# Charging the weight split to the planner's later chains: one hybrid diffusion step on one core

## The chip, the cores and the metric

The kernel runs on one core of a Trainium2 chip. The metric is the device time of one execution in microseconds, the median of several runs.

## What is computed

One inference step of a two-layer network over 640 tokens (128 context tokens and 512 latent tokens) of width 1024. Each layer normalises its input, passes it through one wide input projection to four token mixers, merges their outputs with sigmoid gates, projects, adds, and ends with a SwiGLU network:

```python
h = _rmsnorm(x, norm1_g) * (1 + sc1) + sh1
(aq, ..., mg) = split(h @ w_in)
o_a = _gdn_mixer(...)          # gated DeltaNet, chunked, both directions
o_b = _diff_attend(q_b, keys, vals, lam)   # softmax(map 0) - lam * softmax(map 1)
o_c = _hgrn_mixer(...)         # gated linear recurrence, both directions
o_d = _na_latent(...)          # neighbourhood attention
proj = einsum('btnw,nwd->btnd', branches, w_branch)
x = x + g1 * (einsum('btnd,btnd->btd', sigmoid(mg), proj) @ w_out)
x = x + g2 * swiglu(rmsnorm(x, norm2_g) * (1 + sc2) + sh2)
```

All inputs and results are float32.

## The kernel before

**Products.** A dense product is made of three passes over halves of the numbers. `load_w` fetches a weight tile of 128x1024 numbers (`wraw`), ScalarE rounds it to `whi`, and VectorE subtracts to get the rest, `wlo`. A `unit` then issues three matmuls per 128 rows of the contraction: `whi` by the input's high part, `whi` by its low part, `wlo` by its high part. The inputs are `hh` and `hl` for the normalised input and `mo` for a mixer's output. Their results are the tiles `pu` (320 columns) and `ptk` (256 columns). This dense work is the **fill**.

**Chains.** The four mixers are long sequences of small steps in which TensorE, VectorE and ScalarE take turns. Each is a generator that yields the tiles that its next step on TensorE needs. The list of chains in order of urgency is `prep_a` (rank 0), `mix_a` (1), `mix_d` (2), `mix_c` (3), `mix_b` (4), `prep_b` (5) and `late` (6).

**The planner.** The order on TensorE (PE) is written out by hand. `weave` keeps a rough clock, `now`, of PE's modelled time. It runs a chain's step on PE when the clock has passed the time at which that step's inputs should be ready plus `SLACK` (220 ns); if no chain is due it runs the next piece of fill; if there is neither, the clock jumps. The ready times come from `charge`: each operation of a chain on VectorE or ScalarE adds its modelled cost to a modelled queue of its engine, one queue per rank, and pushes back the queues of all later ranks. The clock and the queues set positions only; no instruction waits for them on the chip.

**VectorE and ScalarE.** Their order is made by a scheduler from priorities. A chain's step has priority `100000 * (8 - rank)`, so 800000 to 600000 for ranks 0 to 2 and 500000 and less for the later ones. The split in `load_w` has `WPRI` = 550000, and stands between them.

**The end of a layer's woven part.** The last fill is `merge`, one per mixer: it multiplies that mixer's output with its part of `w_branch`. The merges come in the order `mix_a`, `mix_c`, `mix_b`, `mix_d`, each when its mixer is done, and `mix_a` and `mix_c` must both be done before the first. `mix_b` works through four heads. Of each head it takes five tiles of tokens (`b_tile`): scores of two maps (`pbs`, twice two rows), VectorE's maxima `b_mx`, ScalarE's exponentials into `be`, sums `b_s`, the combined weights `be` on VectorE, their transposes (`pbt` and the first `pbo`), copies, and the product with the values (the other `pbo`). After the fifth tile a norm (`bo`) and transposes (`goT`) follow, then the store to DRAM from which `merge` loads `moT` and splits it into `mo`.

Of the kernel before, what the change touches and what calls it, by code (L numbers as in the profile page):

```python
# [26 lines left out]
WAIT, WAIT1, FIX, LAT = 150.0, 300.0, 60.0, 270.0  # L27
# [85 lines left out]
class Net:  # L113
# [163 lines left out]
    def load_w(self, src, n=1024, pc=0, raw=None):  # L277

        if raw is None:
            raw = self.wraw.tile([128, 1024], F32, tag="raw", name="wraw")  # L280
        with self.tc.high_priority(offset=DPRI):
            self.nc.sync.dma_start(raw[:, :n], src)
        hi = self.whl.tile([128, 1024], F32R, tag="hi", name="whi")
        lo = self.whl.tile([128, 1024], F32R, tag="lo", name="wlo", bufs=NLO)
        with self.tc.high_priority(offset=WPRI):
            m = n - pc
            self.a.copy(hi[:, :n], raw[:, :n])
            self.v.tensor_tensor(lo[:, :m], raw[:, :m], hi[:, :m].bitcast(F32), ALU.subtract)
            if m < n:
                self.g.tensor_tensor(lo[:, m:n], raw[:, m:n], hi[:, m:n].bitcast(F32), ALU.subtract)  # L290
        return hi, lo
# [1663 lines left out]
```

## Time and profile before

| | |
|---|---|
| time of three runs, median (lowest to highest) | 3421.05 us (3419.64 to 3431.92) |
| the profiled execution, its own time | 3422.57 us |
| its span in the trace | 3420.8 us |
| PE busy in the span | 3325.7 us (97%) |
| VectorE (DVE) busy | 2315.1 us (68%) |
| ScalarE (ACT) busy | 1414.0 us (41%) |
| mean granted clock of TensorE | 0.99 |

PE is the engine to look at: it is busy in all but 95 us, so what the order can still change lies in its gaps and in the stretches in which its clock falls. The granted clock is 1.00 at 2.4 GHz and 0.50 at 1.2 GHz. The two layers' woven parts lie at about 100 to 1180 us and 1780 to 2860 us of the span; between and after them stand the output projection and the SwiGLU network, dense work almost without a gap.

### The profile page before, as it was taken

What the parts mean: (1) busy time and instruction counts of PE and PEld (TensorE: products, weight loads), DVE (VectorE), ACT (ScalarE), POOL (GpSimd) and SP (SyncE); (2) the same over time, 40 slices, a digit from 0 to 9 for tenths busy, and PEclk for the clock granted to TensorE, in tenths of its full rate; (3) what the DMA queues carried; (4) which work ended last, traced back from release to release, by engine and by line L of the source; (5) the groups of instructions that cost most, each with busy time, mean ns of one, the idle gap of its engine ahead of it and who ended that gap; (6) DMA issues with size and microseconds to landing.
All of it is one profiled execution on the core that took longest, in us unless ns stands there. A gap on an engine that the chain in (4) does not pass through costs nothing.

```text
span 3420.8 us, 62210 instructions
## 1 busy us (share of the span) xinstructions
PE 3325.7 (97%) x23732; PEld 3257.6 (95%) x23732; DVE 2315.1 (68%) x5237; ACT 1414.0 (41%) x3162; POOL 222.5 (7%) x385
## 2 busy tenths in 40 slices
PE   8999999999999899999999999999999998999998
PEld 5999999999999899999999999999999998999998
DVE  7689788866666577887456887677556656633435
ACT  5344545545444352222253545555444433422222
POOL 1010000120000000000001101002100100000000
PEclk9999999999999999999999999999999999999999
DMA  6454434675443444544234433356544425322222
GB/s 223 161 167 127 142 125 146 187 226 163 133 138 114 125 157 144 152 152 132 83 122 155 147 124 106 121 147 208 166 123 132 129 70 164 102 70 75 78 77 69
DMA packets 288131, 460.08 MB, mean 134 GB/s; under 512 B 47060, under 2 KB 174676, under 8 KB 287832
## 3 DMA queue, kind: packets, MB, share of 16 engines
q1 hardware_dynamic: 276504, 423.58, 40.0%
q0 software_dynamic: 11328, 32.52, 3.2%
q8 instruction: 187, 3.06, 0.4%
q14 instruction: 112, 0.92, 0.1%
HBM read 368.42 MB, written 87.56 MB: 133 GB/s over the span
## 4 chain that ended last, share of the span: by engine, by line
PE 82%; DVE 7%; DMA 4%; issue 3%; ACT 2%; POOL 1%; SPq 0%; DVEq 0%; ACTq 0%; POOLq 0%
PE pu L151 60%; PE ptk L151 5%; PE pdv L151 1%; PE pW L151 1%; PE pX L151 1%; PE pbs L151 1%; PE pca L151 1%; PE pbo L151 1%; PE pkS L151 1%; PE pdt L157 1%; DVE wlo L106 1%; PE pds L151 1%; PE pao L151 1%; DVE cacc L106 1%; DMA bqk<-rr 1%
## 5 line engine op out<-in xcount | busy, mean ns | idle before, releaser
L151 PE MATMUL pu<-hh,whi 128*128 128x320 f32 (+1 forms) x3760 | 1091.9, 318 | 8.3 <-ACT stg L106 5.1
L151 PE MATMUL pu<-hl,whi 128*128 128x320 f32 (+1 forms) x3760 | 1060.8, 310 | 2.4 <-DVE hl L106 2.4
L151 PE MATMUL pu<-hh,wlo 128*128 128x320 f32 (+1 forms) x3760 | 1061.8, 310 | 0.0
L106 ACT CAST whi<-wraw 128x1024 fp32r<-128x1024 f32 (+2 forms) x410 | 390.5, 953 | 893.8 <-PE pu L151 573.4
L151 PEld LDWEIGHTS pu<-hh,whi 128*128 128x128 f32 (+1 forms) x3760 | 680.1, 188 | 12.7 <-ACT stg L106 5.3
L151 PEld LDWEIGHTS pu<-hl,whi 128*128 128x128 f32 (+1 forms) x3760 | 680.2, 188 | 4.5 <-DVE hl L106 2.6
L151 PEld LDWEIGHTS pu<-hh,wlo 128*128 128x128 f32 (+1 forms) x3760 | 678.9, 187 | 1.7
L106 DVE TENSOR_TENSOR wlo<-wraw,whi 128x1024 fp32r<-128x1024 f32 (+2 forms) x410 | 453.7, 1107 | 299.6 <-ACT whi L106 296.9
L151 PE MATMUL pu<-mo,whi 128*128 128x320 f32 x1024 | 236.7, 319 | 9.6 <-ACT mo L106 9.0
L151 PE MATMUL pu<-fa,whi 128*128 128x320 f32 x1152 | 215.6, 309 | 0.0
L106 DVE SCALAR_TENSOR_TENSOR x<-pu,gn,x 128x128 f32<-128x128 f32 (+1 forms) x336 | 134.0, 434 | 94.0 <-PE pu L151 93.1
L151 PE MATMUL ptk<-whi,hh 128*128 128x256 f32 x640 | 191.2, 299 | 0.0
L151 PEld LDWEIGHTS pu<-mo,whi 128*128 128x128 f32 x1024 | 173.2, 192 | 11.2 <-ACT mo L106 9.7
L151 PE MATMUL ptk<-wlo,hh 128*128 128x256 f32 x640 | 181.5, 284 | 0.5 <-DVE wlo L106 0.5
L151 PE MATMUL ptk<-whi,hl 128*128 128x256 f32 x640 | 181.5, 284 | 0.0
L151 PEld LDWEIGHTS pu<-fa,whi 128*128 128x128 f32 x1152 | 180.8, 188 | 0.0
L151 PE MATMUL pu<-mo,wlo 128*128 128x320 f32 x512 | 160.4, 313 | 0.0
L151 PE MATMUL pu<-fa,wlo 128*128 128x320 f32 x576 | 131.2, 309 | 0.0
L511 DVE CUSTOM_DVE_ANT_0 junk<-wa,cs,bada 128x512 bf16<-128x512 f32 x160 | 120.7, 754 | 5.3 <-DMA wa<-in_wada 2.8
L151 PEld LDWEIGHTS ptk<-wlo,hh 128*128 128x128 f32 x640 | 123.1, 192 | 0.7 <-DVE wlo L106 0.7
L511 DVE CUSTOM_DVE_ANT_0 junk<-wa,cs,mod 128x512 bf16<-128x512 f32 x160 | 119.5, 747 | 5.9 <-DMA wa<-in_wada 3.5
L106 DVE TENSOR_TENSOR fs<-fs,pu 128x320 f32<-128x320 f32 x88 | 39.6, 483 | 123.8 <-PE pu L151 123.8
(422 smaller groups left out, 5924.5 us busy)
## 6 DMA issues: line engine op xcount, KB each, us to landing
wraw<-in_win SPq DMA_DIRECT2D x151, 512.0 KB, 3.8
wa<-in_wada SPq DMA_DIRECT2D x180, 256.0 KB, 3.0
wraw<-in_wg SPq DMA_DIRECT2D x44, 512.0 KB, 3.5
wraw<-in_wu SPq DMA_DIRECT2D x44, 512.0 KB, 3.6
wraw<-in_wd SPq DMA_DIRECT2D x80, 256.0 KB, 2.7
p<-stg SPq DMA_DIRECT2D x112, 160.0 KB, 2.6
wraw<-in_wtok SPq DMA_DIRECT2D x32, 512.0 KB, 3.7
wraw<-in_wbr SPq DMA_DIRECT2D x32, 512.0 KB, 3.5
```

The lines of the kernel that those rows point to most:

```text
L106: r = f(*args, **kw)
L151: r = self.nc.tensor.matmul(out, lhsT, rhs, start=start, stop=stop)
L157: r = self.nc.tensor.transpose(out, src, ident)
L511: self.nc.vector.tensor_tensor_reduce(junk, raw, cs[g], 0.5, o if k0 else self.bada[:, l, m:m + 1], ALU.mult, ALU.add, o)
```

## The change

Every weight tile that is loaded while the planner runs now pushes the modelled queues of ScalarE and VectorE for the ranks 3 to 7, that is for `mix_c`, `mix_b`, `prep_b` and `late`. The costs are the model's own: 60 + 0.84 n ns on ScalarE and 60 + 1.04 n ns on VectorE for n columns. Nothing is added on any engine; the number of instructions stays as it is, and only places move.

```diff
         hi = self.whl.tile([128, 1024], F32R, tag="hi", name="whi")
         lo = self.whl.tile([128, 1024], F32R, tag="lo", name="wlo", bufs=NLO)
+        if self.weaving:
+
+            for key, ns in (('a', 0.84), ('v', 1.04)):
+                q = self.free.setdefault(key, [0.0] * 8)
+                for r in range(3, 8):
+                    q[r] = max(q[r], self.now) + FIX + ns * n
         with self.tc.high_priority(offset=WPRI):
             m = n - pc
             self.a.copy(hi[:, :n], raw[:, :n])
```

**First place: PE at the end of `mix_b` in the first layer**, the last tile of the last head (`pbs` scores, `pbt` and `pbo` transposes, `pbo` values, `goT` transposes of the finished head; `pu` is fill). Before:

```order
L157 MATMUL pbt<-cst_119,be 128x128 x4
L157 MATMUL pbo<-cst_119,be 128x128 x2
L151 MATMUL pu<-mo,whi 128x320 x2
L151 MATMUL pu<-mo,wlo 128x320
...
L151 MATMUL pbo<-bv,be 128x128 x4
L151 MATMUL pbo<-bcx,be 128x128 x2
L151 MATMUL pu<-mo,whi 128x320 x2
L151 MATMUL pu<-mo,wlo 128x320
...
L157 MATMUL goT_13898<-cst_119,bo 128x128
L157 MATMUL goT<-cst_119,bo 128x128 x4
```

And now:

```order
L151 MATMUL pbs<-bKd,bqt 128x512 x2
L151 MATMUL pbs<-bKc,bqt 128x256 x2
L151 MATMUL pbs<-bKd,bqt 128x512 x2
L151 MATMUL pbs<-bKc,bqt 128x256 x2
L157 MATMUL pbt<-cst_119,be 128x128 x4
L157 MATMUL pbo<-cst_119,be 128x128 x2
L151 MATMUL pbo<-bv,be 128x128 x4
L151 MATMUL pbo<-bcx,be 128x128 x2
L157 MATMUL goT_13898<-cst_119,bo 128x128
L157 MATMUL goT<-cst_119,bo 128x128 x4
```

In the order before, the tile's two pairs of scores had 36 matmuls of fill between them, then 60 until `pbt`, 15 until the values and 12 until `goT`. Now the fill has run out: nothing stands between any of these steps. The tile before it has lost its cover too: 15 matmuls between its two pairs of scores, and none until its `pbt` and its values. `goT` itself stands where it stood: in both orders the merges of `mix_a`, `mix_c` and `mix_d` are ahead of it, and only `mix_b`'s own merge is behind.

**Second place: PE at the same end in the second layer.** Before:

```order
L157 MATMUL pbt<-cst_119,be 128x128 x4
L157 MATMUL pbo<-cst_119,be 128x128 x2
L151 MATMUL pu<-mo,whi 128x320 x2
L151 MATMUL pu<-mo,wlo 128x320
...
L151 MATMUL pbo<-bv,be 128x128 x4
L151 MATMUL pbo<-bcx,be 128x128 x2
L151 MATMUL pu<-mo,whi 128x320 x2
L151 MATMUL pu<-mo,wlo 128x320
...
L157 MATMUL goT_33081<-cst_119,bo 128x128
L157 MATMUL goT<-cst_119,bo 128x128 x4
```

And now:

```order
L151 MATMUL pbs<-bKd,bqt 128x512 x2
L151 MATMUL pbs<-bKc,bqt 128x256 x2
L151 MATMUL pbs<-bKd,bqt 128x512 x2
L151 MATMUL pbs<-bKc,bqt 128x256 x2
L157 MATMUL pbt<-cst_119,be 128x128 x4
L157 MATMUL pbo<-cst_119,be 128x128 x2
L151 MATMUL pbo<-bv,be 128x128 x4
L151 MATMUL pbo<-bcx,be 128x128 x2
L157 MATMUL goT_33081<-cst_119,bo 128x128
L157 MATMUL goT<-cst_119,bo 128x128 x4
```

Before, 15 matmuls of fill stood ahead of the values and 24 ahead of `goT`. Now only this last tile stands bare; the tile before it keeps 60 matmuls until its `pbt` and 6 until its values.

**Third place: PE at the end of `mix_d` in the first layer** (`pdt` are the transposes of its weights, one block per head; `pbt` and `pbo` belong to a tile of `mix_b` beside it). Before:

```order
L157 MATMUL pdt<-cst_119,dPl 128x128
L157 MATMUL pdt<-cst_119,dPl 96x128
L157 MATMUL pbt<-cst_119,be 128x128 x4
L157 MATMUL pbo<-cst_119,be 128x128 x2
L151 MATMUL pu<-mo,whi 128x320 x2
L151 MATMUL pu<-mo,wlo 128x320
```

And now:

```order
L157 MATMUL pdt<-cst_119,dPl 128x128
L157 MATMUL pdt<-cst_119,dPl 96x128
L157 MATMUL pbt<-cst_119,be 128x128 x4
L157 MATMUL pbo<-cst_119,be 128x128 x2
L151 MATMUL pbo<-bv,be 128x128 x4
L151 MATMUL pbo<-bcx,be 128x128 x2
```

Before, 21 matmuls of fill stood ahead of the last scores, 21 between these and the first head's `pdt`, and 15 between it and the second head's. Now there is none from the scores on until `mix_d` is done, as it nearly was in the second layer already before the change.

## Rows read from the trace of the kernel before

**Rows 1.** The page, span and first part: busy us, share, instructions.
```profile
span 3420.8 us, 62210 instructions
...
PE 3325.7 (97%) x23732; PEld 3257.6 (95%) x23732; DVE 2315.1 (68%) x5237; ACT 1414.0 (41%) x3162; POOL 222.5 (7%) x385
```

**Rows 2.** Five stretches: us, engines' busy us (instructions), PE clock, DMA share, GB/s.
```profile
200.00:400.00 200.00, 188.19 (x1472) 183.04 (x1471) 176.12 (x378) 97.49 (x222) 16.58 (x30) 0.99 0.44 142
...
1050.00:1100.00 50.00, 47.09 (x332) 46.27 (x331) 30.05 (x78) 18.45 (x46) 0.10 (x1) 1.00 0.37 105
1150.00:1180.00 30.00, 21.41 (x120) 20.50 (x119) 15.54 (x39) 8.20 (x17) 0.00 (x0) 0.77 0.40 123
...
2720.00:2750.00 30.00, 25.07 (x161) 23.23 (x160) 17.98 (x60) 13.99 (x41) 8.51 (x15) 0.89 0.49 143
2830.00:2860.00 30.00, 21.36 (x137) 20.32 (x136) 17.90 (x43) 9.96 (x19) 0.00 (x0) 0.89 0.47 139
```

**Rows 3.** What PE waited for: total us, times, longest us.
```profile
PE goT L157 <- DVE bo L106: 9.8, 3, 5.5
PE pu L151 <- ACT mo L106: 9.0, 2, 6.0
PE pdt L157 <- ACT dPl L106: 6.2, 2, 4.1
...
PE pdt L157 <- DVE b_nm L106: 4.8, 1, 4.8
...
PE pab L157 <- DVE atok L106: 3.9, 2, 2.2
PE pkS L151 <- DVE xp L106: 3.6, 3, 2.0
PE pW L151 <- DVE GT L106: 3.5, 8, 1.4
...
PE pco L151 <- DVE cSS L106: 2.3, 2, 2.1
PE pX L151 <- ACT W L106: 2.1, 2, 1.8
...
PE pbo L151 <- DVE be L106: 1.6, 2, 1.0
```

**Rows 4.** In order of time: the first layer's last `mix_b` tile (start us, us).
```profile
1143.92 0.40 PE L151 MATMUL pbs<-bKc,bqt 128*128 128x256 f32 x2
...
1147.67 1.02 DVE L106 SCALAR_TENSOR_TENSOR be<-be,b_c 128x768 f32<-128x768 f32 x1
...
1152.96 0.60 PE L157 MATMUL pbt<-cst,be 128*128 128x128 f32 x4
```

**Rows 5.** In order of time: a `mix_b` tile without fill, second layer.
```profile
2718.63 1.05 PE L151 MATMUL pbo<-bv,be 128*128 128x128 f32 x8
...
2724.05 0.40 PE L151 MATMUL pbs<-bKc,bqt 128*128 128x256 f32 x2
...
2730.34 1.00 PE L157 MATMUL pbt<-cst,be 128*128 128x128 f32 x4 [1.05 <-DVE be L106]
...
2731.14 0.64 PE L157 MATMUL pbo<-cst,be 128*128 128x128 f32 x2
...
2732.38 2.05 PE L151 MATMUL pbo<-bv,be 128*128 128x128 f32 x8 [0.61 <-DVE be L106]
```

**Rows 6.** In order of time: values to `goT`, first layer, then second.
```profile
1156.71 0.61 PE L151 MATMUL pbo<-bcx,be 128*128 128x128 f32 x4
...
1164.62 1.33 PE L157 MATMUL goT<-cst,bo 128*128 128x128 f32 x5 [5.54 <-DVE bo L106]
...
2834.80 0.61 PE L151 MATMUL pbo<-bcx,be 128*128 128x128 f32 x4
...
2841.07 0.77 PE L157 MATMUL goT<-cst,bo 128*128 128x128 f32 x5 [2.13 <-DVE bo L106]
```

## The prediction, as it was put on record

> **What bounds the kernel now.** I read the page first: PE is busy 3325.7 of 3420.8 us [rows 1], so 95 us of gaps are all that an order can win outright. Then the busy time by stretches. From 200 to 400 us VectorE works 176 of 200 us, and PE loses 12 us of gaps: there the chains wait for VectorE. At the end of `mix_b` the loss is denser: 8.6 of 30 us idle at 1150, at a mean clock of 0.77, and 8.6 of 30 at 2830, at 0.89. The ends of `mix_d` differ: 2.9 of 50 us idle in the first layer at full clock, 4.9 of 30 us in the second, at 0.89 [rows 2]. Then PE's list of waits, which says whose step was late, and last the order of time at the two ends.
>
> The list splits by rank. `pab`, `pkS`, `pW` and `pX` are steps of the ranks 0 and 1: 3.9 + 3.6 + 3.5 + 2.1 = 13.1 us. The change does not charge them. Of the ranks 3 and 4 there is `pco` with 2.3, `pbo` with 1.6 and `goT` with 9.8 us; of `goT`'s three waits the two at the layers' ends are 5.54 and 2.13 us, which leaves 2.1 [rows 3, 6]. So the steps that the change moves later waited some 6 us in all away from the ends. That is the whole direct prize.
>
> **Does a late rank need more time?** One tile shows it. In the first layer's last tile the second scores end at 1143.92 + 0.40 = 1144.32, and the weights are written at 1147.67 + 1.02 = 1148.69: 4.4 us. PE takes up its `pbt` at 1152.96, another 4.3 us later [rows 4]. The 60 matmuls of fill in between took these 8.6 us together, twice what was needed. A later place for such a step removes no wait. It spends fill that is wanted elsewhere.
>
> **The change part by part.** No instruction is added or taken away. The splits stay as they are; the code alone moves steps on PE, and with them what the schedulers of VectorE, ScalarE and the DMA queues put beside them. I cost the last at nothing while dense fill covers them; without fill it counts in the waits below.
>
> *End of `mix_b`, first layer.* Its steps come later while the fill ends where it did, so the last one and a half tiles stand bare.
> - The fourth tile's weights: 4.4 us from the second scores [rows 4] with no fill: 4.4 us idle.
> - Its copies between the transposes and the values: a bare tile waited 0.61 us [rows 5]: 0.6.
> - The fifth tile: both scores stand together, so its two maps queue on VectorE and ScalarE. A tile with its scores side by side and no fill shows 2724.05 + 0.40 to 2730.34, that is 5.9 us [rows 5], though `mix_d`'s last steps ran within it. The single chain's 4.4 us is the lower bound, 5.9 the value and the upper one: 5.9 idle, and again 0.6 for the copies.
> - The norm: from the values' end to `goT` 7.3 us (1157.32 to 1164.62) in the first layer and 5.7 (2835.41 to 2841.07) in the second; in both, work of the merges sits between its small steps on VectorE. Now the fill ends earlier and less of that work is left, so I take 5.7, with 7.3 as the other bound. The 5.54 us of idle before [rows 6] become 5.7: 0.2 more.
>
> Together 4.4 + 0.6 + 5.9 + 0.6 + 0.2 = 11.7 us.
>
> *The same end, second layer.* Only the fifth tile is bare: 5.9 + 0.6, and `goT` goes from 2.13 to 5.7, 3.6 more. Together 10.1 us. What is late behind `goT` in both layers is the store and the load of `mo`, 9.0 us in two waits [rows 3]; both start from `goT`, and I leave them as they are.
>
> *Clock in these ends.* A bare tile also runs slowly: its eight value matmuls took 2.05 us against 1.05 with fill around them [rows 5], the granted clock at 1.2 instead of 2.4 GHz. A tile's other matmuls lose about as much again, so about 2 us a tile, and three tiles give 6 us. The lower bound is nothing (the clock may fall only after them), the upper is 6 plus some 4 us at each end in which the fill behind restarts at 1.2 GHz.
>
> [...]
>
> *End of `mix_d`, first layer.* It becomes what the second layer's end is already: 4.9 us idle in place of 2.9, and a clock of 0.89 over 30 us, 6.6 us at half speed [rows 2], most of it with small matmuls, some 2 us. Together 4; bounds 0 and 6. The second layer's end keeps its form.
>
> *What is won.* The later places end the waits of `pco` and the part of `pbo` outside that end: 2.3 + 1.0 = 3.3 us [rows 3]; `goT`'s 2.1 is already in the account of `mix_d`'s end. Then there is an indirect gain: where VectorE is full (88% of 200 to 400 us), `mix_c`'s work comes some microseconds later and makes room for `prep_a` and `mix_a`. Nothing in the trace before shows how much. The bounds are 0 (these ranks already go first) and all 13.1 us; I take a quarter, 3.3, since they have the higher priority and lose mainly to what has already begun. With 1.4 us for the clock that falls after such gaps this is 8 us; bounds 0 and 3.3 + 13.1 + 1.4 = 18.
>
> *Sum.* 11.7 + 10.1 + 6 + 4 - 8 = 23.8 us. The profiled execution took 3422.57 us, 1.8 more than its span, so 3446.4; it stands 1.5 above the median of the runs, and the forecast is 3445 us.
>
> **Rivals.**
> *Even.* The two ends cost the lower bounds (10.2 and 8.6 us with 4.4 for each tile), the clock in them nothing, `mix_d`'s end nothing, and the middle wins 12: 3421 + 7 = 3428. For it: much of VectorE's load is `mix_c`'s. Against it: the clock at 1150 and 2830 is already low with fewer bare steps.
> *The middle pays it all.* One mechanism: VectorE's full stretches, 200 to 400 us and their like in the second layer. If moving `mix_c` out of them ends the 13.1 us of the ranks 0 and 1, their low clock (0.99 of 200 us, 4 us at half speed, in each layer some 2 us) and the 5.4 us of `pco`, `pbo` and `goT`, and `pdt`'s 6.2 + 4.8 us of `mix_d` [rows 3] go too, 13.1 + 4 + 5.4 + 11.0 = 33.5 us are won against 18.8 lost at the lower bounds: 3406, not slower. It decides from 19 us won, and from 36 it is a gain of over 0.5%. Against it: these chains already precede the others on VectorE.
> *The charge does not do what it says.* It is laid on the queues when a piece of fill begins in the program, while the split is done whenever a buffer comes free, some weights ahead. Then chains move later at places where no split is in their way, the waits in the middle stay, and the restart at low clock comes on top: 3421 + 32 + 8 = 3461. For it: the twofold cover in the tile above.
>
> **How the numbers follow.** The forecast has 0.53, the even case 0.25, the charge that misses 0.13, the middle that pays it all 0.09. About 0.5%, 17 us, is what can be told from no change here: 3404 to 3438. Slower by more than that are the forecast, but for a sixth of it that falls under 3438, and the third rival: 0.44 + 0.13, with a twentieth from the edge of the even case 0.60. Faster is what of the last rival lies beyond 3404, 0.06; 0.34 is left within. The range: the lower bounds of all losses, 18.8, against 18 won give 3422, and with the edge of the last rival 3416; the upper ones, 26.5 for the ends (5.9 for each bare tile, 7.3 for the norm), 14 for the clock and 6, with nothing won, give 3467. I give 3416 to 3465; the likeliest case alone has 3434 to 3460.
>
> **What would show it.** Each step has a place. Right: at both `mix_b` ends `pbt` waits 4 to 6 us for `be`, `goT` waits over 5 us, the granted clock over those 30 us falls below the 0.77 and 0.89 of before, and PE's idle time over the span rises by 10 to 25 us. `mix_d`'s first end looks like the second. Wrong: `pbt` does not appear among PE's waits, or the idle time from 200 to 400 us falls below 6 us. If the ends cost what I say and the time still stays, the middle paid, and PE's list will show `pab`, `pkS` and `pW` gone.

## The result, and the profile after

The changed kernel took 3475.33 us (median of four runs, 3473.89 to 3481.76) against 3421.22 before: a ratio of 1.0153, with a 95% interval of 1.0139 to 1.0168. It is 54 us slower. The forecast was 24 us slower, and the measured time lies 10 us above the end of its range. One execution of the last experiment below ran at a mean clock of 0.65 (4643 us) and is left out of its figures.

The profiled execution of the changed kernel took 3481.76 us, 6 more than its median; the profiles below are of that one. The page, span and first part:

```profile
span 3480.0 us, 62253 instructions
...
PE 3348.9 (96%) x23732; PEld 3276.3 (94%) x23732; DVE 2320.2 (67%) x5237; ACT 1418.5 (41%) x3164; POOL 214.8 (6%) x385
```

Against [rows 1] the span is 59.2 us longer. PE's idle time went from 95.1 to 131.1 us, 36.0 more, and its busy time rose by 23.2 us for the same 23732 matmuls. Over the span the mean granted clock fell from 0.990 to 0.984. The work of VectorE and ScalarE is the same within 5 us.

Busy time by stretches, the columns as in [rows 2], at the places that answer to those rows (the program runs later here, so the stretches do too):

```profile
200.00:400.00 200.00, 190.79 (x1502) 185.91 (x1501) 171.71 (x367) 97.59 (x224) 16.05 (x30) 1.00 0.45 145
1050.00:1100.00 50.00, 45.53 (x297) 43.57 (x297) 32.69 (x87) 20.27 (x53) 9.74 (x17) 0.90 0.39 113
1165.00:1210.00 45.00, 25.50 (x121) 22.95 (x119) 20.57 (x57) 12.18 (x35) 0.00 (x0) 0.73 0.21 67
2755.00:2785.00 30.00, 21.26 (x145) 19.18 (x144) 19.04 (x62) 13.94 (x42) 6.69 (x13) 0.89 0.34 102
2880.00:2915.00 35.00, 20.36 (x99) 18.57 (x98) 16.43 (x45) 10.06 (x26) 0.00 (x0) 0.76 0.31 96
```

At the end of `mix_b` PE is idle 19.5 of 45 us in the first layer and 14.6 of 35 in the second, where it was 8.6 in each [rows 2]. The end of `mix_d` got worse in both layers: 4.5 us idle at a clock of 0.90 in the first, 8.7 of 30 us in the second, which was forecast to stay at 4.9. From 200 to 400 us PE is idle 9.2 us in place of 11.8, and VectorE has 4 us less to do there: an indirect gain may be there, and it is small.

What PE waited for, columns as in [rows 3]:

```profile
PE pbt L157 <- DVE be L106: 20.6, 6, 6.2
PE pds L157 <- ACT dP L106: 10.7, 5, 4.0
PE goT L157 <- DVE bo L106: 7.9, 2, 4.0
...
PE pu L151 <- ACT mo L106: 6.8, 2, 3.5
PE pck L157 <- ACT ckd L106: 5.7, 1, 5.7
PE pco L151 <- DVE cSS L106: 5.3, 3, 3.9
...
PE ppv L151 <- DVE GX L106: 3.6, 1, 3.6
PE pCT L157 <- DVE C L106: 3.4, 1, 3.4
```

`pbt`, the wait that the forecast named, leads the list. But `pco`, which was to go, grew from 2.3 to 5.3. The wait for `dP` of `mix_d`, 1.0 us before, is 10.7, and `ckd` of `mix_c` (5.7 us) and `ppv` and `pCT` of `mix_a` (3.6 and 3.4) are new in the list.

The first layer's last two tiles of `mix_b`, in order of time:

```profile
1170.05 0.40 PE L151 MATMUL pbs<-bKc,bqt 128*128 128x256 f32 x2
...
1171.19 1.22 DVE L106 TENSOR_TENSOR wlo<-wraw,whi 128x1024 fp32r<-128x1024 f32 x1
...
1172.91 1.29 DVE L106 TENSOR_TENSOR mo<-moT,mo 128x320 fp32r<-128x320 f32 x3
...
1176.47 1.09 PE L157 MATMUL pbt<-cst,be 128*128 128x128 f32 x4 [6.02 <-DVE be L106]
...
1178.60 2.05 PE L151 MATMUL pbo<-bv,be 128*128 128x128 f32 x8 [0.61 <-DVE be L106]
...
1183.43 0.63 PE L151 MATMUL pbs<-bKc,bqt 128*128 128x256 f32 x2
...
1189.05 1.08 PE L157 MATMUL pbt<-cst,be 128*128 128x128 f32 x4 [5.00 <-DVE be L106]
...
1191.17 2.05 PE L151 MATMUL pbo<-bv,be 128*128 128x128 f32 x8 [0.61 <-DVE be L106]
...
1198.04 1.33 PE L157 MATMUL goT<-cst,bo 128*128 128x128 f32 x5 [3.96 <-DVE bo L106]
```

Read down the brackets: 6.02 + 0.61 + 5.00 + 0.61 + 3.96 = 16.2 us of idle time. The forecast had 4.4 + 0.6 + 5.9 + 0.6 + 5.7 = 17.2. That the sums are so near is in part luck: the fourth tile took 1.6 us more than forecast, the fifth 0.9 and the norm 1.7 less. In the 6.02 us of the fourth tile VectorE also did 3.9 us of work for the fill (the split `wlo`, parts of `mo`, a step of the merge); in the 5.00 us of the fifth it had none.

### The profile page after: what moved, and what is told of

It reads as the page before. It is cut to its first block, busy times and chain, and to the rows that moved or that the text cites. A ratio compares the mean times of both kernels' runs of the same rounds, so it can differ in the third digit from the quotient of the medians.

```text
span 3480.0 us, 62253 instructions
## 1 busy us (share of the span) xinstructions
PE 3348.9 (96%) x23732; PEld 3276.3 (94%) x23732; DVE 2320.2 (67%) x5237; ACT 1418.5 (41%) x3164; POOL 214.8 (6%) x385
## 4 chain that ended last, share of the span: by engine, by line
PE 78%; DVE 8%; DMA 5%; issue 4%; ACT 3%; POOL 1%; SPq 1%; DVEq 0%; ACTq 0%; POOLq 0%
PE pu L151 58%; PE ptk L151 4%; PE pdv L151 2%; PE pbo L151 1%; PE pbs L151 1%; PE pW L151 1%; PE pX L151 1%; PE pca L151 1%; DVE wlo L106 1%; PE pkS L151 1%; PE pdt L157 1%; DVE cacc L106 1%; PE pds L151 1%; PE pao L151 1%; ACT whi L106 1%
## 5 line engine op out<-in xcount | busy, mean ns | idle before, releaser
L517 DVE CUSTOM_DVE_ANT_0 junk<-wa,cs,mod 128x512 bf16<-128x512 f32 x160 | 119.6, 748 | 10.8 <-DMA wa<-in_wada 8.6
L151 PEld LDWEIGHTS ptk<-whi,hh 128*128 128x128 f32 x640 | 122.5, 191 | 0.0
```

The source lines that it names most:

```text
L151: r = self.nc.tensor.matmul(out, lhsT, rhs, start=start, stop=stop)
L517: self.nc.vector.tensor_tensor_reduce(junk, raw, cs[g], 0.5, o if k0 else self.bada[:, l, m:m + 1], ALU.mult, ALU.add, o)
```

## The experiments

To see where a kernel loses, I numbered the dense matmuls (`pu` and `ptk`), whose sequence is the same in all kernels, and compared the times at which the same ones start. The table gives the loss (or, with a minus, the gain) against the profile of before, in us, by stretches. In the profile of before they are: up to 1018 us, the end of `mix_d` (to 1119), the end of `mix_b` (to 1212), and for the second layer up to 2636, 2803 and 2893 us. The last column is the loss at the last dense matmul. A step of a chain that is moved from one stretch to another takes its PE time along: a tile moved out of an end shows as a loss in the middle, and a tile moved into an end as a gain in the middle. So the 0.1 and 1.1 of the changed kernel hide a loss; the sum is free of this.

| kernel | layer 1 up to there | `mix_d` end | `mix_b` end | layer 2 up to there | `mix_d` end | `mix_b` end | sum |
|---|---|---|---|---|---|---|---|
| changed kernel | 0.1 | 10.0 | 22.3 | 1.1 | 11.6 | 14.9 | 59.9 |
| charge in layer 1 only | -1.7 | 9.2 | 23.6 | -2.3 | -0.4 | 1.1 | 29.5 |
| rank 3 only | 4.4 | 9.4 | 2.8 | 7.3 | 9.6 | 5.0 | 38.5 |
| rank 4 only | 1.1 | 2.6 | 9.6 | -6.1 | 7.8 | 7.1 | 22.0 |
| changed kernel, PE kept busy | -2.2 | 9.3 | 19.5 | 1.8 | 10.9 | 12.1 | 51.2 |
| half the charge | 4.6 | -1.0 | 13.7 | 2.0 | -1.7 | 2.5 | 20.6 |
| ranks 4 up 50 ns earlier | 9.5 | -5.8 | -12.9 | -3.6 | 5.2 | -10.0 | -17.6 |
| ranks 4 up 100 ns earlier | 10.8 | -5.9 | -16.0 | -1.4 | 2.9 | -13.1 | -22.9 |
| ranks 4 up 200 ns earlier | 42.6 | -12.4 | -15.5 | 18.0 | -5.4 | -12.9 | 14.0 |
| ranks 3 up 100 ns earlier | 11.7 | -9.0 | -15.7 | 7.9 | 10.9 | -12.6 | -6.5 |
| changed kernel, ranks 4 up 150 ns earlier | 11.2 | 4.2 | -13.1 | 8.1 | 6.6 | -12.3 | 4.6 |

**The charge in the first layer only.**

```diff
-        if self.weaving:
+        if self.weaving and self.layer == 0:
```

> The charge is laid in the first layer only. Theory A (the fill runs out before the last steps of mix_d and mix_b, and each layer pays at its own ends): the first layer pays as in the changed kernel, where the same matmuls of fill run 32 us later after the layer's end than before, and the second layer is as before; 3421 + 26 to 32 = 3447 to 3453 us, and the order of time after 1800 us is that of the kernel before, shifted. Theory B (the delay of VectorE, ScalarE and the loads is carried through the program): the second layer loses too although its order is the old one; 3460 to 3475 us.

Measured: 3452.56 us, ratio 1.0079 (1.0064 to 1.0095). Theory A's range, and B is out. The first layer pays 31 us as in the changed kernel; the second runs as before. The first layer's `mix_b` end, and the stretches that answer to the second layer's `mix_d` and `mix_b` ends of [rows 2]:

```profile
1165.00:1210.00 45.00, 25.25 (x110) 22.84 (x109) 20.26 (x56) 12.77 (x36) 0.00 (x0) 0.70 0.20 63
2749.00:2779.00 30.00, 25.07 (x164) 23.24 (x163) 18.04 (x60) 14.35 (x43) 8.51 (x15) 0.89 0.50 143
2859.00:2889.00 30.00, 21.96 (x128) 20.64 (x128) 17.22 (x42) 9.34 (x19) 0.00 (x0) 0.77 0.46 132
```

The first end is as bare as in the changed kernel. The second layer's ends have 4.9 and 8.0 us idle, as before the change (4.9 and 8.6); only the clock at the last one is lower, 0.77 in place of 0.89.

**Rank 3 only.**

```diff
-                for r in range(3, 8):
+                for r in (3,):
```

> Only rank 3 (mix_c) is charged. Theory A: mix_b's last tile keeps 33 and 42 matmuls of fill ahead of its pbt (4.8 and 6.2 us against 4.4 needed), so little idle there; goT stands bare, about 0.2 and 3.6 us more than before, the copies 0.6 each, the clock some 2; mix_d's ends lose most of what they lost in the changed kernel (10 and 12 us), some 15 to 20 in all. 3440 to 3448 us. Theory C (the loss comes from mix_c's delay, which holds up the event late and with it all merges by 138 matmuls): as slow as the changed kernel, 3468 to 3480 us. Theory D (mix_b's delay alone makes the loss): no change, 3418 to 3426 us.

Measured: 3463.94 us, ratio 1.0113 (1.0098 to 1.0128), between A and C. A's part on the ends holds: in the table `mix_b`'s cost 2.8 and 5.0 us and `mix_d`'s 9.4 and 9.6. What A did not have is the rest: 12 us lost along the way. PE's waits:

```profile
PE pbt L157 <- DVE be L106: 12.4, 5, 4.4
...
PE pds L157 <- ACT dP L106: 8.0, 5, 3.3
...
PE pCT L157 <- DVE C L106: 3.8, 1, 3.8
```

`pds` is a step of `mix_d` (rank 2) and `pCT` one of `mix_a` (rank 1); neither is charged. `pds` waited 1.0 us before and now waits 8.0, and `pCT`, which was not in the list, 3.8. `pbt` of `mix_b`, not charged here either, went from 1.1 to 12.4, most of it at `mix_d`'s ends and in the second layer's middle. A delay of `mix_c` costs other chains.

**Rank 4 only.**

```diff
-                for r in range(3, 8):
+                for r in (4,):
```

> Only rank 4 (mix_b) is charged. Theory A: mix_b's last tile keeps 12 and 27 matmuls of fill ahead of its pbt (1.8 and 4.0 us against 4.4), so 2.6 and 0.4 us idle, 0.6 for the copies twice, goT 0.2 and 3.6 more, the clock some 3 to 5; mix_d's ends are nearly those of before. 3430 to 3438 us. Theory C (mix_c's delay and late): no change, 3418 to 3426 us. Theory D (mix_b's delay alone): as the changed kernel, 3468 to 3480 us.

Measured: 3444.48 us, ratio 1.0056 (1.0041 to 1.0071): 6 us above A's range, far from C and D. With rank 3 alone at 39 and rank 4 alone at 20 us the two make 59, about the 54 of both. So neither chain is the cause by itself. But they do not cost the same things: in the middles rank 4 adds next to nothing, as the idle times in the part on the prediction show.

**The opposite edit.** The kernel before, with a constant that its model already has:

```diff
-RW, RK = 0.0, 4
+RW, RK = -100.0, 4
```

> The kernel before with the opposite edit: the ranks from 4 on are modelled 100 ns faster for each operation (RW = -100), so mix_b's steps come earlier on PE and 240 and 225 matmuls of fill are left after its last step. Theory A: the waits at mix_b's ends (goT 5.5 and 2.1 us, mo 3.1 and 6.0 us) and the clock that falls there go; the tiles have 4.3 us in hand, so no new waits in the middle: 3395 to 3408 us. The theory that the places before were right for the middle, and that any shift costs there: 3425 us or more.

Measured: 3403.55 us, ratio 0.9939 (0.9922 to 0.9956): faster than both kernels. The two `mix_b` ends gain 16 and 13 us. The first of them, and of the list of waits the longest and `pbt`:

```profile
1140.00:1170.00 30.00, 28.08 (x178) 27.27 (x177) 15.08 (x28) 9.71 (x17) 0.00 (x0) 0.94 0.51 160
```

```profile
PE pdt L157 <- DVE dPl L106: 6.8, 1, 6.8
...
PE pbt L157 <- DVE be L106: 3.3, 2, 2.2
```

1.9 us idle in 30, against 8.6 at this end before [rows 2]; `goT` is gone from the head of the list.

**Keeping PE busy in the bare places.** The changed kernel, with matmuls whose result nobody reads wherever the planner's clock jumps:

```diff
                 assert first is not None, "chains wait for each other"
+                k = int(0.35 * (first - self.now) / 147)
+                if k:
+                    ps, x = self.G1("warm"), self.h[0][0]
+                    for _ in range(k):
+                        self.nc.tensor.matmul(ps[:, :HT], x[:, :128], x[:, :HT], start=True, stop=True)
                 self.now = first
```

> The changed kernel; wherever the planner's clock jumps because nothing is due, PE also runs some matmuls on the normalised input into a tile that nobody reads (about 0.35 of the jump long, some 230 in all, 34 us, in places where PE idled 50 us). They do no useful work. Theory A1 (at the bare ends the clock costs as much as the idle time: in the changed kernel 48.9 us more at 1.2 GHz and 23.2 us more of PE busy for the same matmuls): the ends stay at 2.4 GHz, the time at half clock falls by 30 us or more, and the time is 10 to 20 us under the changed kernel's: 3455 to 3467 us. Theory A2 (the idle time alone decides, or the added matmuls delay the chain's steps as much as they save): 3472 to 3485 us.

Measured: 3473.22 us, ratio 1.0147 (1.0131 to 1.0164), not to be told from the changed kernel's 1.0153. That is A2's range and not A1's, though the clock did what A1 said: over the first layer's end it rose from 0.73 to 0.92.

```profile
1160.00:1205.00 45.00, 36.55 (x230) 34.36 (x229) 22.34 (x60) 13.59 (x37) 0.00 (x0) 0.92 0.25 79
```

The order of time there shows why:

```profile
1167.92 0.40 PE L151 MATMUL pbs<-bKc,bqt 128*128 128x256 f32 x2
1168.16 2.81 PE L227 MATMUL warm<-hh 128*128 128x320 f32 x18
1174.04 0.63 PE L157 MATMUL pbt<-cst,be 128*128 128x128 f32 x4 [3.08 <-DVE be L106]
...
1179.17 1.62 PE L227 MATMUL warm<-hh 128*128 128x320 f32 x10
1180.63 0.63 PE L151 MATMUL pbs<-bKd,bqt 128*128 128x512 f32 x2
...
1192.82 0.76 PE L157 MATMUL goT<-cst,bo 128*128 128x128 f32 x5 [0.61 <-DVE bo L106]
```

From the end of the scores (1168.32) to `pbt` it is 5.7 us, against 6.0 without the added matmuls, at mean clocks of 0.92 and 0.73 over this end: most of this tile's time is VectorE's and ScalarE's. And the ten matmuls between the two pairs of scores put the second pair off by 1.5 us, so that part of what the tile's own matmuls gain at the higher clock (its four `pbt` took 0.63 us in place of 1.09) is given back. From this `pbt` to `goT` it is 18.8 us against 21.6, and in the table each `mix_b` end is 2.8 us shorter. So at each bare end the higher clock, less the delays, is worth some 3 us in these two profiles; over the whole kernel the medians differ by 2 us, which the intervals do not tell from none.

**Half the charge.**

```diff
-                    q[r] = max(q[r], self.now) + FIX + ns * n
+                    q[r] = max(q[r], self.now) + 0.5 * (FIX + ns * n)
```

> The charge at half its size. Theory A (what counts is which of the last steps stand bare): in the first layer mix_b's last tile alone is bare, with two pieces of fill between its scores, in the second layer the end is nearly as before; mix_d's ends are as before; 12 to 18 us at the first end and 2 to 4 at the second: 3435 to 3443 us. Theory P (the loss grows evenly with the charge, since each step is put off by as much): half of 54, 3446 to 3451 us.

Measured: 3439.08 us, ratio 1.0043 (1.0030 to 1.0056): A's range, and under P's. The table has 13.7 and 2.5 us at the two `mix_b` ends, as A said. Under a third of the loss (0.0043 of 0.0153) for half of the charge: it does not grow evenly with the charge, and fits what A says, that it counts which steps are left without fill. A did not have all of it: the longest waits of this run are two of the fill in the middles for `stg`, 11.4 and 6.3 us, where the kernel before waited 5.1 once.

**The opposite edit, twice the size.**

```diff
-RW, RK = 0.0, 4
+RW, RK = -200.0, 4
```

> As the earlier mirror edit, but 200 ns in place of 100 for ranks 4 and up. Theory A: the ends are already covered with 100 ns, so nothing more is won there; mix_d's ends move little. Steps of mix_b come so early that some begin to wait in the middle: 3400 to 3412 us. Theory P (evenly, the other way): another 20 us less than with 100 ns, 3378 to 3388 us.

Measured: 3436.50 us, ratio 1.0038 (1.0025 to 1.0051). Both theories miss. `mix_b`'s ends gain what they gained with 100 ns, as A said; outside them the kernel loses far more than A allowed:

```profile
PE pbt L157 <- DVE be L106: 13.1, 11, 3.8
PE pbt L157 <- DVE grs_y L106: 7.5, 1, 7.5
```

Now `pbt` waits twelve times, none of them at `mix_b`'s last tiles: the 4.3 us in hand [rows 4] were those of one tile late in the layer, and other tiles had less. That a busier VectorE is why was not looked into.

**The opposite edit for `mix_c` too.**

```diff
-RW, RK = 0.0, 4
+RW, RK = -100.0, 3
```

> As the mirror edit with 100 ns, for ranks 3 and up, so that mix_c comes earlier too (its last step after 3999 matmuls of fill in the first layer in place of 4143, 13867 in place of 14462 in the second). Theory A: the first mix_d end, too, is covered better, and the merges start earlier: 3395 to 3405 us, unless mix_c, whose steps take turns with mix_a on a full VectorE from 200 to 400 us, now waits there: then 3405 to 3420 us, with pco, pca or pcs in PE's list of waits.

Measured: 3420.71 us, ratio 0.9988 (0.9977 to 0.9999): A's second case, at the end of its range; nearly all of the gain of 21 us is gone, with longer waits of `mix_c` and of `mix_a` beside it.

```profile
PE pco L151 <- DVE cSS L106: 8.9, 3, 7.2
PE pkS L151 <- DVE xp L106: 7.5, 6, 2.4
PE pab L157 <- DVE atok L106: 6.3, 3, 2.8
```

`pkS` and `pab` had 3.6 and 3.9 us [rows 3]. So the ranks 0 and 1 do lose when `mix_c` comes earlier; that it is VectorE they lose on fits the list, which names it as what they waited for.

**Repair of the ends alone.** The changed kernel with `RW, RK = -150.0, 4`.

```diff
-RW, RK = 0.0, 4
+RW, RK = -150.0, 4
```

> The changed kernel with 150 ns taken off each operation of the ranks from 4 on, so that the charge stays on mix_c but mix_b catches up: 108 and 219 matmuls of fill are left after its last step. Theory A (mix_b's bare ends are the largest part, 27 us of idle time and clock against the kernel before, and another 17 us that the kernel before loses there itself; the rest, in the middle and at mix_d's ends, comes from mix_c's delay and stays): 3425 to 3440 us. Theory E (the loss in the middle also comes from mix_b's places): 3400 to 3412 us. Theory F (the ends matter little): over 3460 us.

Measured: 3426.53 us, ratio 1.0010 (1.0000 to 1.0021): A's range. With `mix_b`'s ends covered again (2.0 and 2.1 us idle) the changed kernel is as fast as before; but it is 23 us slower than the kernel that has the cover, by 100 ns, and no charge. In the table the two differ at `mix_d`'s ends and in the second layer's middle, and little at `mix_b`'s ends. The waits of `pck` and `pds` are those of the charged kernels again, and `pbt` waits at `mix_d`'s ends and in the first layer's middle:

```profile
PE pbt L157 <- DVE be L106: 13.1, 5, 5.1
PE pck L157 <- ACT dPl L106: 7.7, 2, 6.9
PE pds L157 <- ACT dP L106: 6.3, 3, 4.1
```

**The opposite edit at half its size.**

```diff
-RW, RK = 0.0, 4
+RW, RK = -50.0, 4
```

> The mirror edit with 50 ns in place of 100; 105 matmuls of fill are left behind mix_b's last step in each layer. Theory A (the ends need some 7 us of fill behind goT and no more): as with 100 ns, 3398 to 3410 us. Theory P (evenly with the size): half of that gain, 3411 to 3417 us.

Measured: 3404.18 us (median of three), ratio 0.9944 (0.9923 to 0.9964), not to be told from 100 ns: A's range, not P's. Here 105 matmuls behind the last step bought what 240 and 225 did.

## Why the prediction was wrong

**The direction and the main mechanism held.** The fill runs out before `mix_b`'s last steps, PE waits in each of them, and each layer pays by itself. Of the signs that were named, `pbt` waited 5.0 to 6.2 us at both ends and the clock fell to 0.73 and 0.76; `goT` stayed under its 5 us, and the rise in idle time, 36.0 us, is above the 10 to 25. In the first layer the idle time grew by 10.9 us (8.6 to 19.5); the forecast was 11.7. In the second it grew by 6.0 against 10.1: `goT` waited 3.96 us there too, not 5.7, since with the fill gone nothing stood between the norm's small steps on VectorE (first layer, 1194.9 to 1198.0 us), and the wait for `mo` fell as well, 9.0 to 6.8 us for both layers.

**The step that failed first is "What is won".** It was put down as 8 us gained (6.6 of it idle time), with 0 as its lower bound. It is a loss. PE's idle time in the middles went from 16.5 to 22.5 us in the first layer and from 11.2 to 19.3 us in the second, 14 us more, while `pab` and `pkS` did get better (3.9 to 0.6 and 3.6 to 2.2 us). Both middles, before and after:

```profile
333.00:1018.00 685.00, 668.46 (x4981) 658.64 (x4982) 514.83 (x1234) 337.11 (x813) 72.53 (x118) 0.99 0.52 158
2014.00:2636.00 622.00, 610.84 (x4604) 602.60 (x4602) 428.99 (x972) 307.64 (x743) 75.69 (x115) 1.00 0.47 143
...
331.00:1018.00 687.00, 664.46 (x4909) 654.52 (x4908) 504.77 (x1187) 327.57 (x778) 72.46 (x114) 0.98 0.51 155
2041.00:2670.00 629.00, 609.75 (x4556) 600.27 (x4555) 423.73 (x941) 309.36 (x727) 65.00 (x106) 0.99 0.46 139
```

The same stretches of the other runs say whose delay it is. Idle time in both middles together: 27.7 us before, 41.8 in the changed kernel, 42.6 with rank 3 alone, 29.0 with rank 4 alone, 41.8 in the repair. So the loss comes from `mix_c`'s delay; `mix_b`'s alone adds 1.3 us.

I took the waits of before as a list from which a later place can only strike lines. But a later step meets another neighbour, and `mix_a` and `mix_d`, which are not charged, wait too (`pCT`, `ppv`, `pds`). One of the new waits shows how, on ScalarE and VectorE of the changed kernel, in order of time:

```profile
2456.27 0.60 PE L157 MATMUL pck<-cst,cQS 128*128 128x128 f32 x4
2456.66 1.22 DVE L106 TENSOR_TENSOR rr<-rr,rot 128x1024 f32<-128x1024 f32 x1 [8.89 <-DMA rr<-qk]
...
2460.24 1.04 ACT L106 CAST rr<-rx 128x1024 fp32r<-128x1024 f32 x1 [6.02 <-DVE rx L106]
2461.19 0.43 ACT L106 ACTIVATE mth<-pu 128x320 f32<-128x320 f32 x1
2461.52 0.36 ACT L106 COPY dvw<-pdv 96x256 f32<-96x256 f32 x1
2461.77 0.27 ACT L106 COPY csn<-pcs 128x128 f32<-128x128 f32 x1
2461.93 0.59 ACT L106 COPY ckd<-pck 128x512 f32<-128x512 f32 x1
...
2462.58 0.48 PE L157 MATMUL pck<-cst,cQS 128*128 128x128 f32 x1 [5.70 <-ACT ckd L106]
```

`rr` belongs to `prep_b`, rank 5. VectorE waited for its load, ScalarE for VectorE, and behind it on ScalarE stood copies of `mix_d` and `mix_c` for which PE had done its part: the last of it, `pck`, by 2456.9 us, and the copy `ckd` began at 2461.93, 5.1 us later. They had to wait for a less urgent chain, and PE, whose next step needed `ckd`, with them: ScalarE sat idle for 6.02 us before the cast of `rr`, and `ckd`, ready for the last 3.4 of these, ran only behind it. Whether the other new waits come about in the same way was not followed.

**The second is "the second layer's end keeps its form".** At `mix_d`'s ends the forecast was 4 us in the first layer and none in the second. The idle time grew from 2.9 to 4.5 us and from 4.9 to 11.6 us over the stretches of the table, and the clock fell in both. The second layer's order looked alike in the last steps, which I compared; but it had been short of fill before, and the transposes and values of one more tile of `mix_b` now stand among the bare steps. With rank 3 alone these ends lose nearly the same, 9.4 and 9.6 us in the table, so `mix_c`'s delay is enough to empty them. In the second layer rank 4 alone does nearly as much, 7.8 us: there either delay is enough.

**The third is the clock, a term that was mis-sized.** It was 6 us at `mix_b`'s ends and 2 at `mix_d`'s, less 1.4 in the middles, a number for which no row was given. None was given either for the 4 us of restart at each end, in its upper bound and in the third rival; in the clock records PE stands at 0.50 from `goT` on for 13.7 and 6.8 us before the change, and for 6.8 and 10.2 us after it. PE's busy time rose by 23.2 us. The time at a granted clock of 0.50, added up from the traces' clock records, went from 66 to 115 us, 49 more: some 20 more at `mix_b`'s ends, 14 at `mix_d`'s and 20 in the middles, where the forecast had a gain, and 5 less elsewhere. PE was busy in 44.1 of the 66 us and in 86.5 of the 115, 42.4 more. In these two traces matmuls of 320 columns start 147 ns apart at 1.00 and 266 at 0.50, those of 256 columns 120 and 213, those of 128x128 111 and 213. From this come two estimates. The 64 columns more take 27 and 53 ns, 2.4 and 1.2 columns a nanosecond, which agrees with the forecast's 2.4 and 1.2 GHz. And the 42.4 us hold work that takes 22 to 23 us at 1.00, so that 19 to 20 of the 23.2 us are the clock's. Yet the clock follows from the waits (each of the 20 stretches at 0.50 in the changed kernel's records begins 2.3 to 4.4 us after PE began a wait of 1.9 us or more) and is not won back by itself. With added matmuls the time at 0.50 fell to 74 us and PE's busy time without them by 13 us, but the rest of the span grew by 5, and the medians show 2 us, within their noise.

So the shortfall against the span's 59.2 us adds up, in us: middles 14.0 more idle in place of 6.6 less, `mix_d`'s ends 8.2 in place of 2, `mix_b`'s ends 16.9 in place of 21.8, PE's busy time 23.2 in place of the clock's 6.6, and 3.1 less idle elsewhere. The middles and the busy time, most of it the clock's, are the bulk of it.

Of the rivals, the third (no gain in the middle, and the restart at low clock, 3461 us) came nearest, and still 14 us short, because it took the middle's gain as nothing where it was a loss. Its reason, that the charge falls at places where no split is in the way, no run here tests. The even case and the one in which the middle pays failed on the same step. In the chances, 0.44 + 0.13 and a twentieth of the even case's 0.25 make 0.58, not 0.60; nothing here hangs on it.

The reading of one tile, that its step came 4.3 us later than it had to already, pointed the right way: putting rank 4 earlier by 50 to 100 ns an operation wins some 20 us. It did not hold for all tiles, as the run with 200 ns shows.

What stays open: why just these steps wait. That `mix_c`'s delay makes the 14 us in the middles is shown; which part of it any such delay would cost, and which is the chance of who meets whom, is not. The half charge and the opposite edits each show another set of waits there, and no run holds the neighbours fixed while it moves one chain.

## What to carry to other kernels

Where an engine, as PE here (97% busy), is kept full by independent work between the steps of long chains, that work is a stock: put off a chain and it is used up earlier, and the chain's last steps stand bare at their full latency, here 5.0 to 6.2 us from a tile's scores to its transposes. So look at the end of the slowest chain first, and count what is left behind its last step; 105 matmuls were enough here, and 240 and 225 bought nothing more. And bound the gain of a later place below zero: a moved step does not only leave its old neighbours, it also stands in front of new ones, and here a chain of low rank that waited for a load held a copy of a higher one for 5.1 us.

## What the runs showed of the hardware

A bare tile of `mix_b` took 5.0 to 6.2 us from its second scores to its transposes; the one tile that was followed at the higher clock took 5.7 there, at a mean of 0.92 over that end, and 6.0 without, at 0.73. While ScalarE waited 6.02 us for one operand, a copy behind that instruction whose input was ready for the last 3.4 of them did not run. At a granted clock of 0.50 a tile's eight value matmuls took 2.05 us, in place of 1.05 at 1.00 [rows 5]. In the gaps of a kernel that waits for other engines, 234 added matmuls of some 0.31 us lifted the mean clock from 0.984 to 0.989, and its time did not change beyond the noise.
